# Head norms of the projection: one operand of every root step in PSUM

## The chip, the cores and the metric

The kernel runs on one core of a Trainium2 chip. That core has a matrix engine (TensorE, written PE; its weight loads PEld), three engines for element-wise work (VectorE = DVE, ScalarE = ACT, GpSimd = POOL), and an engine that mostly issues transfers (SyncE = SP). All work on SBUF, the core's large memory of 128 partitions; PE writes its results into PSUM, a small second memory of eight banks, which DVE and ACT can also read and write. The metric is the device time of one execution in microseconds; the kernel before takes 3017.64 us (median of 3 runs, 3017.33 to 3021.18).

## What is computed

One step of a two-layer network on 1024 latent tokens and 128 context tokens, with 1024 features each. Every layer has a normalisation with modulation, a projection `h @ w_in` into parts for a convolution branch and two attention branches, the three branches, an output projection and a two-step MLP. All of it is float32; the matrix products are made of three products of split operands, so that they keep about float32 precision.

The change touches one piece of that, the norm of each attention head. The projection's columns for queries and keys are cut into heads of 64, and each is divided by its root mean square:

```
def _rms(x, g):
    xf = x.astype(jnp.float32)
    y = xf * lax.rsqrt(jnp.mean(xf * xf, axis=-1, keepdims=True) + EPS)
    return (y * g.astype(jnp.float32)).astype(x.dtype)
...
    qa = _rms(qa.reshape(B, L, GQA_HEADS, HEAD_DIM), aqg)
    ka = _rms(ka.reshape(B, L, GQA_KV_HEADS, HEAD_DIM), akg)
    qn = _rms(qn.reshape(B, L, NA_HEADS, HEAD_DIM), nqg)
    kn = _rms(kn.reshape(B, L, NA_HEADS, HEAD_DIM), nkg)
```

## The kernel before

The program is written in one fixed order: each engine executes its instructions in the order in which the Python code emits them, and Python generators (`yield`, `next`) interleave the pieces by hand. A framework adds the semaphores between engines. Tiles come from pools: the pools S, T, U and V in SBUF, and eight PSUM buffers of one bank each (`P`), which are handed out again as they come free.

A layer begins with its norm (`norm1`), goes on to the projection (`project`), then the two attentions (`gqa`, `natten`), the output projection and the MLP. The projection works in column blocks of 256: V0 and V1 feed the convolution, A0 to A5 hold queries, keys and some values, VN values. Each of A0 to VN is walked in five token groups (`GROUPS`): four of two 128-token tiles (48 matmuls each) and one, the context tokens, of one tile (24 matmuls). For each group, in this order:

- PE multiplies (`tok_group`, L541 to L543) into a PSUM tile `pst`.
- In groups 1 and 3, the next weight half-block is split into a high and a low part (`wh` by ACT, `wl` by DVE), and another is fetched (`wr`).
- The first half of `post` calls `head_stats`: ACT squares (`sq`), DVE sums over each head (`ss`, L420), ACT takes Ln and Exp (`y`, by `rsq_start`). A tile of n = 2, 4 or 8 numbers per partition results.
- One step of the convolution follows (`conv_taps`): one or two taps on DVE (`cacc`, L102) for one half of the channels, and for the other half one tap by ACT (`cp`) and POOL (`cacc`, L570), from the end of block A1 on. POOL's part has 22 taps, DVE's the rest.
- The second half of `post` calls `head_norm`: three small DVE steps improve the root (`rsq_end`, through L102), one DVE multiplication applies it (`xn`, L99), and POOL multiplies by gains or rotates (`o`, L471 to L490).
- In every second group, one step of the modulation (`fill`) runs: PE multiplies a weight row block (`aw`) into `psmod`; when a modulation is complete, DVE copies `psmod` to `mt` (L229) and PE transposes it (`psmt`, L233).
- SP issues the transfers (all through L144): weights `wr`, modulation weights `aw`, and the stores of `o` to DRAM buffers (`ddA`, `dvA`), each three groups after it was noted.

The VN block has no head norm, so there are 30 norms in a layer and 60 in all. From block A5 on, the grouped attention's start is interleaved as well: it loads the keys back from DRAM (`kd`), and PE transposes them (`pstr`, L784).

The root is computed in two parts. `rsq_start` (ACT) makes y = exp(-0.5 ln(ss/64 + eps)), an approximate reciprocal root. `rsq_end` (DVE) makes one Newton step: t = y*y*(-0.5/64), t = (ss + 64 eps)*t, y = (t + 1.5)*y. All of y, t and ss are small tiles of pool V in SBUF. The same two helpers serve the other norms, which the change leaves alone.

Of the kernel before, what the change touches and what calls it, by code (L numbers as in the profile page):

```python
# [14 lines left out]
ACTF = mybir.ActivationFunctionType  # L15
ALU = mybir.AluOpType
# [9 lines left out]
DH = 64  # L26
EPS = 1e-6
# [18 lines left out]
def hybrid_step(ctx, tc, I, O, depth=DEPTH):  # L46
# [7 lines left out]
    def nm(p):  # L54
        count[0] += 1
        return f"{p}{count[0]}"
# [4 lines left out]
    def T(shape, dt=F32, n="t"):  # L61
        return pers.tile([128] + list(shape), dt, tag="T", bufs=N_T, name=nm(n))
# [4 lines left out]
    def V(shape, n="v"):  # L67
        return pers.tile([128] + list(shape), F32, tag="V", bufs=24, name=nm(n))
# [18 lines left out]
    def P(n="ps"):  # L87
        return psum.tile([128, 512], F32, tag="p", bufs=8, name=nm(n))
# [3 lines left out]
    def act(out, in_, func, scale=1.0, bias=0.0, **k):  # L92
        nc.scalar.activation(out=out, in_=in_, func=func, scale=scale, bias=bias, **k)  # L93
# [4 lines left out]
    def tt(out, a, b, op, eng=None):  # L98
        (eng or nc.vector).tensor_tensor(out=out, in0=a, in1=b, op=op)  # L99

    def stt(out, a, s, b, op0, op1):
        nc.vector.scalar_tensor_tensor(out=out, in0=a, scalar=s, in1=b, op0=op0, op1=op1)  # L102
# [7 lines left out]
    eps = pers.tile([128, 1], F32, name="eps")  # L110
# [51 lines left out]
    def rsq_start(q, y, m):  # L162

        act(y, q, ACTF.Ln, scale=1.0 / m, bias=eps)
        act(y, y, ACTF.Exp, scale=-0.5)

    def rsq_end(q, y, t, m):

        stt(t, y, -0.5 / m, y, ALU.mult, ALU.mult)
        stt(t, q, EPS * m, t, ALU.add, ALU.mult)  # L170
        stt(y, t, 1.5, y, ALU.add, ALU.mult)
# [239 lines left out]
    def heads4(a, nt):  # L411

        return a.rearrange("p t (h d) -> p t h d", d=64)

    def head_stats(x, nt):
        n = nt * (x.shape[2] // 64)
        sq = T([nt, x.shape[2]], n="sq")
        act(sq, x, ACTF.Square)
        ss = V([n], "ss")
        nc.vector.tensor_reduce(out=ss, in_=sq.rearrange("p t (h d) -> p (t h) d", d=64), op=ALU.add, axis=AX.X)  # L420
        y = V([n], "y")
        rsq_start(ss, y, DH)
        return x, nt, n, ss, y

    def head_norm(x, nt, n, ss, y):
        rsq_end(ss, y, V([n], "nt"), DH)
        w = x.shape[2]
        xn = T([nt, w], n="xn")
        tt(heads4(xn, nt), heads4(x, nt), y.rearrange("p (t h) -> p t h", t=nt).unsqueeze(3).to_broadcast([128, nt, w // 64, 64]), ALU.mult)
        return xn  # L430
# [61 lines left out]
    def post(L, c, t, nt, ps):  # L492
# [5 lines left out]
        if normed is not None:  # L498
            st = head_stats(x[:, :, normed], nt)
# [4 lines left out]
        if normed is not None:  # L504
            xn = head_norm(*st)
            if c in ("A0", "A1"):
                post_rope(L, c, t, nt, xn, o)
            else:
                gain(o[:, :, normed], xn, 2 if c in ("A2", "A3") else 3, nt, L)
# [1463 lines left out]
```

## Time and profile before

| what | value |
|---|---|
| median of 3 runs | 3017.64 us |
| the profiled execution's own time | 3022.51 us |
| its span, first to last instruction | 3020.7 us |
| mean granted TensorE clock | 0.972 |
| busy PE / DVE / ACT / POOL | 2857.6 / 2085.0 / 1403.4 / 650.5 us |
| projection of layer 0, about 109 to 345 us: busy PE / DVE / ACT / POOL | 221.3 / 176.5 / 80.4 / 148.4 us |
| projection of layer 1, about 1610 to 1845 us: busy PE / DVE / ACT / POOL | 221.3 / 180.4 / 81.2 / 143.0 us |

All durations and places come from the one profiled execution; its own time stands 4.87 us above the median of the others. A row of a timeline has the start, the duration, the engine, the line and the operation, the tile written and the tiles read, the shapes and, in brackets, the idle time before it with what ended that. L93, L96, L99, L102 and L106 are helpers (activation, ACT copy, two-operand step, scalar-and-two-tensor step, tensor-scalar step), so the tile's name tells which work it is. In lists of waits, the first name is who waited and the second what ended the wait.

### The profile page before, as it was taken

How to read it: one execution, taken by the hardware profiler on the slowest of the kernel's cores; microseconds unless marked ns; L12 is line 12 of the kernel's file. 1: busy time of each engine (PE TensorE's matmuls, PEld its weight loads, DVE VectorE, ACT ScalarE, POOL GpSimd, SP SyncE). 2: the span in 40 equal slices, each digit the busy share in tenths (PEclk: the TensorE clock that was granted, in tenths of full speed). 3: DMA queues.
4: the chain of work that ended last, by engine and by line, in shares of the span. 5: the costliest groups of instructions: out<-in, count | busy, mean ns of one | idle time of the engine just before them, and what ended most of it. 6: DMA issues, size and time to landing. Idle time of an engine off the chain costs nothing.

```text
span 3020.7 us, 52765 instructions
## 1 busy us (share of the span) xinstructions
PE 2857.6 (95%) x20328; PEld 2540.2 (84%) x20328; DVE 2085.0 (69%) x3985; ACT 1403.4 (46%) x2880; POOL 650.5 (22%) x607
## 2 busy tenths in 40 slices
PE   6998999999889999999889999999997999999999
PEld 3878745799789999999878886458997999999999
DVE  6587778864767556758665877778557775585676
ACT  4334356763644444433452343568435444434344
POOL 3576345410000000000225762463100000000000
PEclk7999999999999999999989999999998999999999
DMA  7276302423466658443433671024334654575334
GB/s 282 82 209 172 97 24 55 101 81 114 134 197 200 207 165 297 162 154 95 139 122 98 186 205 59 16 59 105 95 119 155 194 174 158 174 253 175 126 96 164
DMA packets 424124, 430.42 MB, mean 142 GB/s; under 512 B 120000, under 2 KB 299968, under 8 KB 423872
## 3 DMA queue, kind: packets, MB, share of 16 engines
q1 hardware_dynamic: 423872, 427.04, 45.4%
q8 instruction: 160, 2.62, 0.4%
q14 instruction: 92, 0.75, 0.1%
HBM read 298.50 MB, written 128.45 MB: 141 GB/s over the span
## 4 chain that ended last, share of the span: by engine, by line
PE 74%; DVE 14%; ACT 4%; DMA 2%; issue 2%; POOL 2%; SPq 1%; DVEq 0%; POOLq 0%; ACTq 0%
PE ps L1319 23%; PE psa L1319 8%; PE psc L1319 7%; PE pso L1319 5%; PE psb L1319 5%; PE psacc L1118 3%; PE pspv L985 2%; DVE cacc L102 2%; PE psd L1319 2%; PE pspt L969 2%; PE psst L1132 2%; PE psm L1044 2%; PE pst L541 1%; PE pst L542 1%; PE pst L543 1%
## 5 line engine op out<-in xcount | busy, mean ns | idle before, releaser
L1319 PE MATMUL ps<-ts,w2h 128*128 128x288 f32 x3072 | 534.4, 296 | 8.3 <-DVE ts L99 4.8
L1319 PEld LDWEIGHTS ps<-ts,w2h 128*128 128x128 f32 x3072 | 451.7, 189 | 9.2 <-DVE ts L99 5.3
L1319 PE MATMUL ps<-ts,w2l 128*128 128x288 f32 x1536 | 329.2, 295 | 0.1
L96 ACT CAST ts<-ti 128x576 fp32r<-128x576 f32 x256 | 172.1, 672 | 314.4 <-PE ps L1319 216.4
L541 PE MATMUL pst<-wh,HA 128*128 128x256 f32 x1040 | 298.8, 287 | 0.0
L542 PE MATMUL pst<-wl,HA 128*128 128x256 f32 x1040 | 295.8, 284 | 0.0
L543 PE MATMUL pst<-wh,HA 128*128 128x256 f32 x1040 | 294.7, 283 | 0.0
L93 ACT ACTIVATE ev<-ev 128x576 f32<-128x576 f32 x224 | 153.7, 686 | 275.0 <-DVE ev L99 271.4
L1319 PEld LDWEIGHTS ps<-ts,w2l 128*128 128x128 f32 x1536 | 247.4, 189 | 0.4 <-DVE w2l L99 0.3
L99 DVE TENSOR_TENSOR ts<-ti,ts 128x576 fp32r<-128x576 f32 x256 | 194.6, 760 | 48.4 <-ACT ts L96 47.6
L102 DVE SCALAR_TENSOR_TENSOR X<-ps,mod,X 128x288 f32<-128x288 f32 x336 | 112.1, 408 | 161.4 <-PE ps L1319 161.4
L541 PEld LDWEIGHTS pst<-wh,HA 128*128 128x128 f32 x1040 | 199.6, 192 | 19.8 <-issue 7.6
L542 PEld LDWEIGHTS pst<-wl,HA 128*128 128x128 f32 x1040 | 199.3, 192 | 0.1
L543 PEld LDWEIGHTS pst<-wh,HA 128*128 128x128 f32 x1040 | 199.3, 192 | 0.0
L99 POOL TENSOR_TENSOR nacc<-nacc,nsq 128x512 f32<-128x512 f32 (+1 forms) x12 | 15.9, 1322 | 836.4 <-PE ps L1319 810.4
L1762 POOL COPY yu<-X 128x128 f32<-128x128 f32 x8 | 3.9, 499 | 855.2 <-DVE X L102 843.2
L99 DVE TENSOR_TENSOR w1l<-w1r,w1h 128x512 fp32r<-128x512 f32 x128 | 87.7, 689 | 133.6 <-ACT w1h L96 130.2
L1319 PE MATMUL pso<-HA,woh 128*128 128x288 f32 x1024 | 177.6, 295 | 0.0
L1046 DVE TENSOR_REDUCE mx<-psm 128x1 f32<-128x384 f32 x288 | 142.2, 546 | 31.9 <-PE psm L1044 31.7
L93 ACT ACTIVATE pt<-psst 128x512 f32<-128x512 f32 x216 | 118.2, 597 | 90.9 <-PE psst L1133 89.9
L99 POOL TENSOR_TENSOR R<-R,pt 128x1024 f32<-128x1024 f32 x60 | 148.3, 2472 | 27.9 <-ACT pt L93 25.9
L1319 PEld LDWEIGHTS pso<-HA,woh 128*128 128x128 f32 x1024 | 149.6, 188 | 0.0
(279 smaller groups left out, 7290.2 us busy)
## 6 DMA issues: line engine op xcount, KB each, us to landing
ti<-hd SPq DMA_DIRECT2D x128, 576.0 KB, 4.0
hd<-ev SPq DMA_DIRECT2D x224, 288.0 KB, 3.8
aw<-in_ada_w SPq DMA_DIRECT2D x160, 256.0 KB, 3.8
w1r<-in_mlp_w SPq DMA_DIRECT2D x160, 256.0 KB, 4.4
HF<-in_mlp_w SPq DMA_DIRECT2D x128, 256.0 KB, 5.1
ddA<-o SPq DMA_DIRECT2D x144, 128.0 KB, 2.9
wr<-in_w_in SPq DMA_DIRECT2D x28, 512.0 KB, 4.0
qd<-ddA SPq DMA_DIRECT2D x48, 256.0 KB, 3.3
```

The lines of the kernel that those rows point to most:

```text
L93: nc.scalar.activation(out=out, in_=in_, func=func, scale=scale, bias=bias, **k)
L96: nc.scalar.copy(out, in_)
L99: (eng or nc.vector).tensor_tensor(out=out, in0=a, in1=b, op=op)
L102: nc.vector.scalar_tensor_tensor(out=out, in0=a, scalar=s, in1=b, op0=op0, op1=op1)
L541: mm(o, hi, wh, start=(k == 0), stop=False)
L542: mm(o, hi, wl, start=False, stop=False)
L543: mm(o, lo, wh, start=False, stop=(k == KT - 1))
L969: nc.tensor.transpose(ps[0:n, c], self.p[j][:, o:o + n], ident)
L985: mm(ps[64 * j:64 * j + 64, 0:128], v[j], self.at[j, i], start=(i == 0), stop=(i == nb - 1))
L1046: nc.vector.tensor_reduce(out=mx[j][:, qt, b:b + 1], in_=ps[:, 0:384], op=ALU.max, axis=AX.X)
L1118: mm(acc[64 * j:64 * j + 64, :], v, pt[:, j, :], start=(kt == 0), stop=(kt == 8))
L1319: mm(ps[h][:, 0:HH], x, y[:, h * HH:(h + 1) * HH], start=(start and z == 0), stop=(stop and z == 2), skip_group_check=True)
```

## The change

`head_stats` and `head_norm` no longer use the two helpers. `head_stats` takes one more PSUM buffer (`pss`) and cuts two small pieces from it, z and t. ACT computes the approximate root twice from the same logarithm: into z in PSUM and into y in SBUF. The three DVE steps are the same arithmetic with other operands: t (PSUM) from y (SBUF) and z (PSUM); z (PSUM) from ss (SBUF) and t (PSUM); y (SBUF) from z (PSUM) and y (SBUF). The V tile `nt` goes away.

```
         y = V([n], "y")
-        rsq_start(ss, y, DH)
-        return x, nt, n, ss, y
-
-    def head_norm(x, nt, n, ss, y):
-        rsq_end(ss, y, V([n], "nt"), DH)
+        small = P("pss")
+        z, t = small[:, 0:n], small[:, 64:64 + n]
+        act(y, ss, ACTF.Ln, scale=1.0 / DH, bias=eps)
+        act(z, y, ACTF.Exp, scale=-0.5)
+        act(y, y, ACTF.Exp, scale=-0.5)
+        return x, nt, n, ss, y, z, t
+
+    def head_norm(x, nt, n, ss, y, z, t):
+
+        stt(t, y, -0.5 / DH, z, ALU.mult, ALU.mult)
+        stt(z, ss, EPS * DH, t, ALU.add, ALU.mult)
+        stt(y, z, 1.5, y, ALU.add, ALU.mult)
         w = x.shape[2]
```

## The prediction

> **What bounds the kernel now.** I first read the busy time of each engine over the two projection stages, where all 60 head norms run, 30 in each layer.
>
> ```profile
> 109.00:345.00 236.00, 221.34 (x1741) 198.55 (x1739) 176.45 (x238) 80.41 (x164) 148.42 (x118) 0.97 0.62 169
> 1610.00:1845.00 235.00, 221.28 (x1711) 195.01 (x1710) 180.37 (x243) 81.21 (x163) 143.04 (x113) 0.97 0.61 166
> ```
>
> After the stretch and its length stand the busy times of PE, PEld, DVE, ACT and POOL, then the granted clock. PE is busy for 221 of 235 us: TensorE is the bound, and DVE time counts only where it makes PE wait. So I asked next what PE waited for in these stretches (total, times, longest), layer 0 and then layer 1.
>
> ```profile
> PE psmod L224 <- DMA aw<-in_ada_w: 5.8, 5, 1.9
> PE psmt L233 <- DVE mt L229: 5.7, 1, 5.7
> PE pstr L784 <- DMA kd<-ddA: 3.1, 1, 3.1
> ```
>
> ```profile
> PE psmt L233 <- DVE mt L229: 5.5, 1, 5.5
> PE psmod L224 <- DMA aw<-in_ada_w: 3.3, 4, 1.6
> PE pstr L784 <- DMA kd<-ddA: 2.6, 1, 2.6
> ```
>
> That is 14.6 us and 11.4 us: in each layer one long wait for a DVE copy (mt, the modulation result), one for the first keys read back (kd), and short ones for modulation weights (aw). Behind the two long ones PE runs slowly for a while:
>
> ```profile
> 245.20:249.30 4.10, 4.10 (x20) 4.10 (x21) 3.95 (x6) 1.84 (x4) 0.61 (x2) 0.50 0.60 128
> 249.40:253.50 4.10, 4.10 (x37) 4.10 (x36) 4.07 (x4) 1.78 (x5) 4.10 (x2) 1.00 0.02 6
> 291.20:297.10 5.90, 5.90 (x28) 5.90 (x29) 2.48 (x6) 4.18 (x7) 3.98 (x3) 0.50 1.04 297
> 1739.40:1744.30 4.90, 4.90 (x24) 4.90 (x25) 4.74 (x8) 1.94 (x4) 1.35 (x2) 0.50 0.50 107
> 1785.40:1788.70 3.30, 3.30 (x16) 3.30 (x17) 2.46 (x6) 1.69 (x4) 1.81 (x2) 0.50 1.00 290
> ```
>
> At clock 0.50, 20 matmuls fit into the 4.1 us that hold 37 at clock 1.00 (0.111 us each). The four slow stretches therefore lose 4.1-20x0.111 = 1.9, 5.9-28x0.111 = 2.8, 4.9-24x0.111 = 2.2 and 3.3-16x0.111 = 1.5 us. They follow the mt, kd, mt and kd waits.
>
> **The change, part by part.** The three steps of the root now take all tensor inputs from SBUF. The listings by tile show what such steps cost (minimum/median/maximum in ns):
>
> ```profile
> L93 ACT ACTIVATE y<-y x60: 203/208/211, 119.7 to 1804.7; 128x8 f32<-128x8 f32 x32, 128x4 f32<-128x4 f32 x24, 128x2 f32<-128x2 f32 x4
> L102 DVE SCALAR_TENSOR_TENSOR nt<-y x60: 146/168/2690, 122.7 to 1804.9; 128x8 f32<-128x8 f32 x32, 128x4 f32<-128x4 f32 x24, 128x2 f32<-128x2 f32 x4
> L99 DVE TENSOR_TENSOR xn<-pst,y x60: 290/690/693, 123.2 to 1809.6; 128x512 f32<-128x512 f32 x32, 128x256 f32<-128x256 f32 x24, 128x128 f32<-128x128 f32 x4
> L99 DVE TENSOR_TENSOR mod<-psmt,vecs x12: 156/164/174, 46.1 to 1854.9; 128x16 f32<-128x16 f32 x12
> L102 DVE SCALAR_TENSOR_TENSOR A<-mod,vecs x8: 151/166/2116, 46.3 to 1857.1; 128x8 f32<-128x8 f32 x8
> L102 DVE SCALAR_TENSOR_TENSOR rt<-rr,pssum x12: 670/676/687, 398.4 to 2067.0; 128x512 f32<-128x512 f32 x12
> L102 DVE SCALAR_TENSOR_TENSOR cacc<-cin,vecs,cacc x78: 1417/1450/3710, 135.7 to 1853.5; 128x1167 f32<-128x1167 f32 x78
> ```
>
> A norm step of 0.165 us sometimes takes 2.7. So do other steps with two SBUF inputs: A, and the convolution taps cacc. Steps with one PSUM input never do: xn runs right behind the norm and never passes 0.693, mod keeps to 0.156-0.174, and rt is the changed steps' own instruction with SBUF first and PSUM second. The cause stands in the timeline, DVE and then POOL:
>
> ```profile
> 280.23 1.54 DVE L102 SCALAR_TENSOR_TENSOR nt<-y 128x4 f32<-128x4 f32 x1 [0.60 <-ACT y L93]
> 281.80 1.21 DVE L102 SCALAR_TENSOR_TENSOR nt<-ss,nt 128x4 f32<-128x4 f32 x1
> 283.05 2.63 DVE L102 SCALAR_TENSOR_TENSOR y<-nt,y 128x4 f32<-128x4 f32 x1
> 285.81 0.42 DVE L99 TENSOR_TENSOR xn<-pst,y 128x256 f32<-128x256 f32 x1
> ```
>
> ```profile
> 279.05 2.70 POOL L570 TENSOR_TENSOR cacc<-cacc,cp 128x1167 f32<-128x1167 f32 x1 [1.33 <-DMA aw<-in_ada_w]
> 281.71 1.28 POOL L471 TENSOR_TENSOR o<-xn,gains 128x512 f32<-128x512 f32 x1
> 282.95 2.71 POOL L570 TENSOR_TENSOR cacc<-cacc,cp 128x1167 f32<-128x1167 f32 x1
> ```
>
> Each step ends just as a POOL instruction ends: three POOL instructions, three steps. How much that is, by the busy time of the norm steps alone, in layer 0's projection and in the stretch before its mt wait:
>
> ```profile
> 109.00:345.00 236.00, 47.44 (x90) 0.97 0.62 169
> 209.00:239.40 30.40, 11.93 (x12) 1.00 0.55 154
> ```
>
> Unstalled, 90 steps take 90x0.165 = 14.9 us; the other 32.5 us are stall, in layer 0 alone. The change takes this off DVE; from PE it takes nothing by itself.
>
> *Added.* One Exp into PSUM per norm. Into SBUF it takes 0.21 us; an Exp written to PSUM is not in the trace. In order behind the other Exp it lengthens the chain by 0 to 0.21 us; I take 0.15, nearest to the SBUF row. ACT is busy for 80 of 236 us, so this hides in its waiting time; were ACT full, it would cost 60x0.21 = 12.6 us. The DVE steps' price in PSUM: the nearest rows are mod (0.164, one PSUM input) and A (0.166, none), so 0 +- 0.02 us each, at most 180x0.02 = 4 us of DVE, on no path of PE.
>
> The Trainium skill's Perfetto Trace Analysis (Optimizing Scalar/DVE Operations) puts DVE's fixed access cost at about 60 ns in SBUF and 125 ns in PSUM, which speaks against the change: as an estimate, 180x65 ns would put 11.7 us more on DVE. The rows mod and A show no such difference in the length of an instruction.
>
> *The mt wait.* The work of DVE just before it, and the taps' busy time by themselves up to there (DVE's is 15.48 us for 8 taps, POOL's 14.99 for 5):
>
> ```profile
> 237.28 5.84 DVE L102 SCALAR_TENSOR_TENSOR cacc<-cin,vecs,cacc 128x1167 f32<-128x1167 f32 x2
> 244.29 0.68 DVE L229 COPY mt<-psmod 128x512 f32<-128x512 f32 x1
> ```
>
> ```profile
> 209.00:244.40 35.40, 0.00 (x0) 0.00 (x0) 15.48 (x8) 0.00 (x0) 14.99 (x5) 0.97 0.54 145
> ```
>
> An unhindered tap takes 1.43 us, so 8 need 11.5 and wait 4.0. The 12 norm steps wait 11.93-12x0.165 = 9.9. Without that, DVE reaches the next tap, or the next weight split wl, earlier; these keep two SBUF inputs and will meet POOL in its place. Following the order by hand, with POOL's tap at 2.7 us, its gain at 1.3 and the waiting engine next in turn, taps and splits wait about 6 us in place of 4. DVE is then 9.9-2 = 8 us earlier at mt, and 5.7 are enough. So I take the whole wait off, 5.7 and 5.5, and the slow clock behind it, 1.9 and 2.2: **15.3 us**. Bounds: 0 if the taps take back all of it, 15.3 if they take back under 4.
>
> *The kd wait.* The norm quoted at 280.23 takes 5.4 instead of 0.55 us, so its xn comes 4.9 earlier. SP issues in order, and its loads and stores wait for such an xn and for POOL's outputs behind it:
>
> ```profile
> 277.74 2.15 SPq L144 DMA_DIRECT2D ddA<-o  x4
> 279.99 3.36 SPq L144 DMA_DIRECT2D aw<-in_ada_w  x4
> 283.40 2.80 SPq L144 DMA_DIRECT2D ddA<-o  x4
> 286.30 0.62 SPq L144 DMA_DIRECT2D kd<-ddA  x1
> ```
>
> ```profile
> 1777.21 2.20 SPq L144 DMA_DIRECT2D ddA<-o  x4
> ```
>
> In layer 0 the 3.36 and 2.80 can shrink to 2.15, what four issues took just before. Then kd leaves 1.9 us earlier, and the slow clock (2.8) goes with most of the wait. In layer 1 the issues ahead of kd are hardly hindered (2.20 for four); I take 1.0 of the 2.6 and keep the slow clock. **5.7 us**; bounds 0 and 3.1+2.8+2.6+1.5 = 10.0.
>
> *The aw waits* (9.1 us) lie mostly where the stalls are still short. I take **1 us**; bounds 0 and 9.1.
>
> Sum: 15.3+5.7+1 = 22 us off the profiled execution's own 3022.51, 3000.5. That execution stood 4.87 above the median of the runs, 3017.64; against the median the forecast is **2996**.
>
> *PSUM.* One more of 8 buffers per norm, held until its third step; psmod holds one throughout. Seven buffers at two per group still let PE be three groups ahead of the norms. I cost it at nothing; its price if that is wrong is rival (d).
>
> **Rivals.**
>
> (a) *The stall moves to the taps.* DVE leaves the norm early and stands as long in the next tap or split. For it: the pair at 237.28 already loses 5.84-2.86 = 3.0 us. Against: a norm meets POOL up to three times, a pair of taps twice. With half of the mt wait kept and all its slow clock, 11.2/2+1 = 7 us are gained: 3011. The Trainium skill's SBUF — State Buffer (Who interferes with whom) has the shared port locked for a whole instruction, this rival's mechanism; the timeline above agrees.
>
> (b) *All three waits go*, because SP and POOL come as early as DVE: 15.3+10.0+6 = 31 us, 2986. Against: SP issues back to back in layer 1.
>
> (c) *No effect*: PE's waits follow POOL's taps and SP's issues and only DVE's idle time grows, or a PSUM input does not free the steps: 3018. For it: POOL is busy for 148 of 236 us, and the stores wait for it. Against: mt waits for DVE alone.
>
> (d) *Slower: PE waits for a PSUM buffer.* If only two groups' worth turn over, PE may start a group only when the norm of the last but one is done. A group of two tiles is 48 matmuls, 5.3 us. The norm would run some 7 us behind it (an estimate: Square, sums, Ln and Exp 2, taps 2.9, their wait 1, steps and xn 1.2), so 1.7 us for each of the 32 such groups in blocks A1 to A4 of both layers: 54 us, less the 22, 3050. It decides once a norm runs further behind than one group. Against: the lists of PE's waits hold no wait for a buffer.
>
> **How the numbers follow.** Forecast 0.54, (a) 0.16, (b) 0.12, (c) 0.10, (d) 0.08. A measurement of this kernel tells about 0.2%, 6 us, from no change. Faster: the forecast, (b) and most of (a), 0.79. Within 0.2%: (c) and the rest of (a), 0.13. Slower: 0.08. The range runs from (b) with a little more of the aw waits to just past (a), 2982 to 3014; (c) and (d) lie outside.
>
> **What would show it.** Norm steps never over 0.25 us and their 47 us in layer 0 near 15; longer means on cacc and wl; the psmt waits gone and clock 1.00 where they were; layer 0's kd wait below 1.5 us. If norm steps still reach 2.6 us, a PSUM input does not free DVE and the forecast falls. If they are short and psmt still waits over 3 us, it is (a) or (c). If the weight loads of pst wait for DVE and the projection grows, it is (d).

## The result, and the profile after

The changed kernel takes **2996.61 us** (median of 4 runs, 2994.11 to 3002.31); the kernel before, timed beside it, 3019.41 us (4 runs, 3017.33 to 3024.02). The ratio is 0.9925, with a 95% interval of 0.9906 to 0.9944: a gain of 22.8 us. The forecast was 22 us off the 3017.64 us of the three earlier runs of before, that is 2996. The time is right; the experiments show that one of the steps to it was not.

The profiled execution of the changed kernel has a time of its own of 2996.72 us and a span of 2994.9; that of before, 3022.51 and 3020.7. Compare first the two projections, from the first to the last matrix product of the blocks. Before, by stretches: length, then busy PE, PEld, DVE, ACT and POOL, then the granted clock.

```profile
109.30:343.90 234.60, 219.94 (x1731) 198.13 (x1730) 175.57 (x238) 80.04 (x163) 148.42 (x118) 0.97 0.62 170
1603.80:1837.20 233.40, 221.96 (x1731) 198.31 (x1729) 176.95 (x239) 81.29 (x164) 148.14 (x118) 0.97 0.61 166
```

After:

```profile
107.20:328.20 221.00, 215.87 (x1730) 193.51 (x1729) 147.69 (x238) 86.18 (x193) 150.46 (x118) 1.00 0.66 180
1588.00:1808.10 220.10, 215.00 (x1731) 194.21 (x1729) 148.15 (x239) 87.17 (x194) 152.79 (x118) 1.00 0.65 176
```

Layer 0's projection is 13.6 us shorter and layer 1's 13.3, together 26.9. The same number of matmuls keeps PE busy for 4.1 us less in layer 0 and for 7.0 less in layer 1. Most of that is the slow clock, which is gone (0.97 to 1.00). By the working of the prediction its four stretches cost 1.9+2.8 = 4.7 us in layer 0 and 2.2+1.5 = 3.7 in layer 1. Layer 1 had a third stretch, behind short waits for aw:

```profile
1645.40:1648.80 3.40, 3.35 (x6) 0.17 (x4) 3.18 (x5) 1.44 (x3) 3.32 (x4) 0.51 0.92 226
```

At half the clock it loses 1.7 of its 3.4 us. Another 1.6 of the 7.0 us are not placed. The rest of the gain, 9.5 and 6.3 us, is PE idle before (234.60-219.94 = 14.7 and 11.4) that is not idle any more (5.1 and 5.1). The prologue, which the change does not touch, was 2.1 us shorter in this execution: from 88 to 93 us the granted clock was 0.66 in the profile of before and is 1.00 here. The kernel before without POOL's taps (one of the experiments below), whose prologue is the same as before, also has 1.00 there, so this is not the change's doing. 26.9+2.1 less the 25.8 between the spans leaves 3.2 us given back after layer 1's projection. Of the 25.8, 3.1 come from the profiled execution of before standing above its median here (3022.51 against 3019.41).

One profiled execution against one other is therefore rough by a few us. The closest neighbour of the changed kernel is the first experiment below, the same instructions with z and t in SBUF. Its projections take 231.8 and 231.6 us (107.5 to 339.3 and 1602.5 to 1834.1), and the changed kernel's are 22.3 us shorter than these: 8.8 us of busy PE and 13.5 us of idle PE.

The waits of PE in the projections after (total, times, longest), layer 0, then layer 1:

```profile
PE psmod L224 <- DMA aw<-in_ada_w: 4.5, 6, 1.5
PE psnm L1042 <- DVE nmx L1036: 2.3, 1, 2.3
PE pstr L791 <- DMA kd<-ddA: 0.7, 1, 0.7
```

```profile
PE psmod L224 <- DMA aw<-in_ada_w: 4.5, 4, 1.5
PE psmu L736 <- DVE cacc L102: 3.2, 1, 3.2
PE psnm L1042 <- DVE nmx L1036: 2.3, 1, 2.3
PE pstr L791 <- DMA kd<-ddA: 0.6, 1, 0.6
```

The wait at mt (psmt, 5.7 and 5.5) has left both lists, kd is down from 3.1 and 2.6 to 0.7 and 0.6, and aw stands at 9.0 in all (9.1 before). The waits named psnm and psmu belong to the start of attention.

The norm steps by themselves, in the two projections (DVE, then ACT's new Exp), and by tile (minimum/median/maximum in ns):

```profile
107.00:340.00 233.00, 14.81 (x90) 5.37 (x30) 0.99 0.63 174
1590.00:1825.00 235.00, 14.83 (x90) 5.36 (x30) 0.99 0.62 169
```

```profile
L93 ACT ACTIVATE pss<-y x60: 175/180/181, 117.6 to 1775.8; 128x8 f32<-128x8 f32 x32, 128x4 f32<-128x4 f32 x24, 128x2 f32<-128x2 f32 x4
L102 DVE SCALAR_TENSOR_TENSOR pss<-y,pss x60: 151/162/172, 120.5 to 1776.2; 128x8 f32<-128x8 f32 x32, 128x4 f32<-128x4 f32 x24, 128x2 f32<-128x2 f32 x4
L102 DVE SCALAR_TENSOR_TENSOR pss<-ss,pss x60: 165/170/173, 120.7 to 1776.4; 128x8 f32<-128x8 f32 x32, 128x4 f32<-128x4 f32 x24, 128x2 f32<-128x2 f32 x4
L102 DVE SCALAR_TENSOR_TENSOR y<-pss,y x60: 159/166/166, 120.9 to 1776.6; 128x8 f32<-128x8 f32 x32, 128x4 f32<-128x4 f32 x24, 128x2 f32<-128x2 f32 x4
```

None of 180 steps passes 0.173 us, where some took 2.7; layer 0's 47.4 us became 14.8. DVE is now idle, by the first table, for 73 of 221 us in layer 0. Around mt the timeline of DVE reads:

```profile
229.46 3.41 DVE L102 SCALAR_TENSOR_TENSOR cacc<-cin,vecs,cacc 128x1167 f32<-128x1167 f32 x2
232.79 0.16 DVE L102 SCALAR_TENSOR_TENSOR pss<-y,pss 128x8 f32<-128x8 f32 x1
...
234.05 0.68 DVE L229 COPY mt<-psmod 128x512 f32<-128x512 f32 x1
```

mt is copied at 234.05 in place of 244.29, and the pair of taps ahead of it takes 3.41 us in place of 5.84.

### The profile page after: what moved, and what is told of

It is laid out like the page before. It is cut to its first block, busy times and chain, and to the rows that moved or that the text cites. A ratio compares the mean times of both kernels' runs of the same rounds, so it can differ in the third digit from the quotient of the medians.

```text
span 2994.9 us, 52825 instructions
## 1 busy us (share of the span) xinstructions
PE 2843.5 (95%) x20328; PEld 2529.8 (84%) x20328; DVE 2030.1 (68%) x3985; ACT 1416.0 (47%) x2940; POOL 656.1 (22%) x607
## 4 chain that ended last, share of the span: by engine, by line
PE 77%; DVE 10%; ACT 4%; POOL 3%; DMA 2%; issue 2%; SPq 1%; DVEq 0%; POOLq 0%; ACTq 0%
PE ps L1326 23%; PE psa L1326 8%; PE psc L1326 7%; PE pso L1326 5%; PE psb L1326 5%; PE psacc L1125 3%; PE pst L548 3%; PE pst L549 3%; PE pst L550 3%; PE pspv L992 2%; PE psd L1326 2%; PE pspt L976 2%; PE psst L1139 2%; PE psm L1051 1%; PE pstr L791 1%
## 5 line engine op out<-in xcount | busy, mean ns | idle before, releaser
L548 PE MATMUL pst<-wh,HA 128*128 128x256 f32 x1040 | 295.3, 284 | 0.0
L550 PE MATMUL pst<-wh,HA 128*128 128x256 f32 x1040 | 291.7, 280 | 0.0
L548 PEld LDWEIGHTS pst<-wh,HA 128*128 128x128 f32 x1040 | 195.8, 188 | 19.2 <-PE pst L550 5.2
L550 PEld LDWEIGHTS pst<-wh,HA 128*128 128x128 f32 x1040 | 196.0, 188 | 0.0
L102 DVE SCALAR_TENSOR_TENSOR cacc<-cin,vecs,cacc 128x1167 f32<-128x1167 f32 x78 | 138.5, 1775 | 18.6 <-POOL cacc L577 17.4
```

What stands on the lines that cost most here:

```text
L548: mm(o, hi, wh, start=(k == 0), stop=False)
L550: mm(o, lo, wh, start=False, stop=(k == KT - 1))
```

## The experiments

Each kernel was timed beside the kernel before; the ratio is to that. They undo one part of the change, do one part alone, or price one wait. The short diffs are against the changed kernel, except where the text says that a kernel is made from the one before.

### The change with z and t in SBUF

```
-        small = P("pss")
-        z, t = small[:, 0:n], small[:, 64:64 + n]
+        z, t = V([n], "z"), V([n], "tn")
```

> The change as it is, but z and t are two small SBUF tiles instead of pieces of a PSUM buffer; the second Exp and the order of the steps stay. Theory (a step with two SBUF inputs waits for POOL, one with a PSUM input does not): the stall is back, norm steps again reach 2.6 to 2.7 us and sum to about 47 us in a projection, PE waits 5 to 6 us for mt in each layer, and the time is that of the kernel before, 3014 to 3022 us. Rival (the gain comes from the new form of the chain, a separate z and t instead of steps in place): norm steps stay near 0.17 us and the time near 2997 us.

Measured: 3020.85 against 3020.31, ratio 1.0004 (0.9994 to 1.0013). The same instructions in the same order, but for the place of two small tiles, gain nothing. The stall is back, a little smaller than expected: the norm steps take 42.9 us in layer 0 and 43.9 in layer 1, PE waits 4.0 and 3.8 us at mt and 4.0 and 2.5 at kd, and the longest step is again 2675 ns:

```profile
L102 DVE SCALAR_TENSOR_TENSOR tn<-y,z x60: 148/278/2675, 120.8 to 1802.4; 128x8 f32<-128x8 f32 x32, 128x4 f32<-128x4 f32 x24, 128x2 f32<-128x2 f32 x4
```

The place in PSUM is the whole gain.

### The new Exp alone

```
-        stt(t, y, -0.5 / DH, z, ALU.mult, ALU.mult)
-        stt(z, ss, EPS * DH, t, ALU.add, ALU.mult)
-        stt(y, z, 1.5, y, ALU.add, ALU.mult)
+        rsq_end(ss, y, V([n], "nt"), DH)
```

> Only what the change adds: the second Exp into a PSUM buffer is made and read by nobody, and the three steps are those of the kernel before, in SBUF. Theory: ACT has room, so 60 more instructions of about 0.18 us (11 us of ACT) cost nothing on PE's path: 3015 to 3023 us, with the mt and kd waits as before. Rival (the longer chain delays every norm, and the change gained more than was seen): 3 to 10 us slower than before, up to 3029 us.

Measured: 3020.93, ratio 0.9999 (0.9990 to 1.0008). The Exp into PSUM, 0.18 us each, costs nothing that can be measured.

### Blocks A0 to A3 alone, and A4 and A5 alone

Two kernels; in the second the list is `("A4", "A5")`. The other blocks keep the old steps.

```
+        if not new:
+            rsq_start(ss, y, DH)
+            return x, nt, n, ss, y, None, None
...
+        if z is None:
+            rsq_end(ss, y, V([n], "nt"), DH)
+        else:
...
-            st = head_stats(x[:, :, normed], nt)
+            st = head_stats(x[:, :, normed], nt, c in ("A0", "A1", "A2", "A3"))
```

> The change in blocks A0 to A3 alone, the old steps in A4 and A5. Theory (time is gained only at the waits of PE behind which the stall stands): the mt waits (5.7 and 5.5 us) and the slow clock behind them (1.9 and 2.2 us) go, the kd waits stay at 2 to 3 us: 15 us gained, 3000 to 3007 us. Rival (kd waits for the whole backlog of DVE and SP, not for block A4's norms): the kd waits go as well, below 1 us, and the time is near 2997 us.

> The change in blocks A4 and A5 alone, the old steps in A0 to A3. Theory: the mt waits stay at 5 to 6 us in each layer with clock 0.50 behind them, the kd waits fall below 1 us and the clock behind them is 1.00: about 2.4+2.0+2.8+1.5 = 9 us gained, 3008 to 3013 us; with the run on A0 to A3 it adds up to the change's 23 us. Rival (kd follows the backlog from the earlier blocks): the kd waits stay above 2 us and the time within 3 us of the kernel before.

Measured: A0 to A3 give **2998.62**, ratio 0.9924 (0.9912 to 0.9935), the whole gain and more than the theory allowed; A4 and A5 give 3021.30, ratio 1.0004 (0.9995 to 1.0013), nothing, though their norm steps do not stall any more (0.172 us at most). With A4 and A5 alone kd is issued at 283.66, 2.6 us earlier than before, and yet PE stands 2.9 us in front of the same transposes (put down there to the norm's xn) and then 3.1 us for the last taps (psmu), a wait that the profile of before does not have in layer 0. The step of the prediction that took 5.7 us at kd from the stall of one norm of A4 (quoted at 280.23) falls. DVE, then POOL and SP, in layer 0 with only A0 to A3 changed:

```profile
269.81 1.54 DVE L102 SCALAR_TENSOR_TENSOR nt<-y 128x4 f32<-128x4 f32 x1 [0.60 <-ACT y L93]
271.38 1.21 DVE L102 SCALAR_TENSOR_TENSOR nt<-ss,nt 128x4 f32<-128x4 f32 x1
272.63 2.62 DVE L102 SCALAR_TENSOR_TENSOR y<-nt,y 128x4 f32<-128x4 f32 x1
275.37 0.42 DVE L99 TENSOR_TENSOR xn<-pst,y 128x256 f32<-128x256 f32 x1
```

```profile
271.29 1.28 POOL L484 TENSOR_TENSOR o<-xn,gains 128x512 f32<-128x512 f32 x1
...
272.98 2.36 SPq L144 DMA_DIRECT2D ddA<-o  x4
275.43 1.70 SPq L144 DMA_DIRECT2D kd<-ddA  x1
```

The norm stalls exactly as before, 5.4 us, but the stores ahead of kd leave at 272.98, before the norm's xn at 275.37: they do not wait for this norm. What they follow is POOL's gain for an earlier group, which ends at 272.57, 10.4 us earlier than before (281.71+1.28 = 282.99); kd is issued 10.9 us earlier (275.43 against 286.30) and PE waits for it 1.8 us in place of 3.1, and not at all in layer 1. The rows of the prediction could have said so: there, too, the stores at 283.40 begin before that norm's xn at 285.81. kd is set by how late the earlier blocks left DVE and POOL.

### Blocks A2 and A3 alone, and A3 alone

The same edit with `c in ("A2", "A3")`, and with `c == "A3"`.

> The change made in blocks A2 and A3 alone (10 of the 30 norms of a layer); A0, A1, A4 and A5 keep the old steps. In layer 0 before, DVE is busy for only 3.6 of the 10 us from 190 to 200 us, which is in A2's first two groups, and over 95% from there to the wait at mt. Theory: a stall counts only if DVE has no idle time between it and the place where PE waits, so A0's and A1's stalls (4.4 us over 10 norms) are made good anyway and A2 and A3 (16.3 us) bring all of the gain: 2996 to 3001, no wait at mt. Rival: every stall ahead of the wait counts alike, 16.3 of 20.7 us: a gain of 17 of 21.7 us, 3002 to 3006, with some wait left at mt or kd.

> The change made in block A3 alone: 5 norms of a layer, of which three lie ahead of the wait at mt in layer 0 and stall 5.1 us there; A2's five norms with 7.8 us of stall keep the old steps. Theory: stalls count in proportion once DVE has no idle time: 5.1 us removed, one or two taken back by taps and wl, leave 1.5 to 3 us of wait at mt and some of the wait at kd: 3004 to 3012. Rival: a few us are all it takes, and A3 brings the whole gain: 2995 to 3001.

Measured: A2 and A3 **2995.67** against 3019.80, ratio 0.9912 (0.9897 to 0.9928); A3 alone **3003.21** against 3020.44, ratio 0.9947 (0.9934 to 0.9959); each lies just below the lower end of its theory. So 10 of the 30 norms of a layer bring all of the gain; A0 and A1, ahead of a stretch in which DVE is busy for 3.6 of 10 us, need no change. Five norms bring 17 us. Their waits in layer 0's projection (then the start of attention), A2 and A3 first, A3 alone second:

```profile
PE psmod L224 <- DMA aw<-in_ada_w: 3.3, 3, 1.7
PE psnm L1048 <- DVE nmx L1042: 2.3, 1, 2.3
PE pstr L797 <- DMA kd<-ddA: 1.7, 1, 1.7
```

```profile
PE psmod L224 <- DMA aw<-in_ada_w: 5.3, 6, 1.7
PE pstr L797 <- DMA kd<-ddA: 2.7, 1, 2.7
...
PE psmt L233 <- DVE mt L229: 0.9, 1, 0.9
```

With A3 alone the wait at mt of 5.7 us shrinks to 0.9 and kd stays at 2.7; with A2 as well, mt goes and kd falls to 1.7. The first microseconds taken off DVE's delay serve mt, the next ones kd. The slow clock behind kd shrinks already with A3 alone: about 3.4 us at 0.50 in layer 0, none in layer 1. In medians that is 17.2 us with A3 alone (12 to 20 by its interval), and 5 to 7 more with A2 or with the whole change.

### The wait at mt taken away by itself

The kernel before, with the transposes of mt issued one step of the modulation later; what follows them in the modulation, the clearing of the next psmod first of all, moves a step later with them:

```
             nc.vector.tensor_copy(mt, ps)
             yield
+            if not first:
+                yield
             pt = P("psmt")
```

> The kernel before, norm steps untouched (they stall as before); only the transposes of mt on PE are issued one step of the modulation later (some 10 us), so PE does not stand at mt. Theory: the wait at mt is where DVE's delay first reaches PE; DVE, ACT and POOL stay as late as they were, so without that stop PE arrives about 5.6 us earlier at the keys (kd) and waits there for most of what it saved: kd waits 3.1 -> 6 to 9 us and 2.6 -> 5 to 8 us, time 3013 to 3019. Rival (the sum of my prediction, which priced each wait by itself): the mt wait and its slow clock go, kd stays near 3, time 3003 to 3008.

Measured: 3024.26 against 3019.80, ratio 1.0009 (0.9998 to 1.0019). No gain, against a sum that prices each wait by itself (3003 to 3008). The time lies above the theory's range too, and PE did not stop where the theory put it. Layer 0's projection:

```profile
PE psmod L224 <- DVE psmod L219: 10.1, 1, 10.1
PE psmod L224 <- DMA aw<-in_ada_w: 4.7, 5, 1.8
```

DVE around the place:

```profile
268.57 0.90 DVE L102 SCALAR_TENSOR_TENSOR nt<-y 128x8 f32<-128x8 f32 x1 [0.61 <-ACT y L93]
269.51 1.20 DVE L102 SCALAR_TENSOR_TENSOR nt<-ss,nt 128x8 f32<-128x8 f32 x1
270.74 2.57 DVE L102 SCALAR_TENSOR_TENSOR y<-nt,y 128x8 f32<-128x8 f32 x1
273.41 0.69 DVE L99 TENSOR_TENSOR xn<-pst,y 128x512 f32<-128x512 f32 x1
274.21 0.48 DVE L219 MEMSET psmod<- 128x512 f32 x1
```

PE runs past mt and stops at the next thing it needs from DVE, the clearing of the next psmod, for 10.1 us in place of 5.7; in layer 1 it stops at a weight split (wl, 5.7) and at psmod (2.7). kd does not grow (no wait in layer 0, 2.0 us in layer 1), since DVE's delay is met ahead of it. The wait at mt is a symptom: the delay on DVE is what costs, and it is paid at the next handover.

### Only the first step with an operand in PSUM

```
-        stt(t, y, -0.5 / DH, z, ALU.mult, ALU.mult)
-        stt(z, ss, EPS * DH, t, ALU.add, ALU.mult)
-        stt(y, z, 1.5, y, ALU.add, ALU.mult)
+        v = V([n], "nt")
+        stt(v, y, -0.5 / DH, z, ALU.mult, ALU.mult)
+        stt(v, ss, EPS * DH, v, ALU.add, ALU.mult)
+        stt(y, v, 1.5, y, ALU.add, ALU.mult)
```

> Only the first of the three norm steps keeps an operand in PSUM (it reads z there); the second and third read and write SBUF again. In the kernel before, the three steps of layer 0's projection took 19.8, 11.2 and 16.4 us, unhindered 5 us each. Theory: a step waits for the POOL instruction that runs beside it, so what step 1 no longer waits for, step 2 meets instead; only the POOL instruction that would have been met first is sometimes over by then. Norm steps 36 to 46 us in layer 0 (before 47.4, after 14.8), the wait at mt stays between 2 and 5 us, time 3008 to 3018. Rival: the steps wait independently of each other, so the first one's 14.9 us of stall just go: norm steps 32 to 34 us, the wait at mt under 1.5 us, time 3000 to 3007. Full gain (2996) would say that one PSUM operand is enough.

Measured: 3016.03 against 3019.80, ratio 0.9985 (0.9975 to 0.9996). The time and the wait at mt (3.2 and 2.9 us) are the theory's, the length of the steps (33.0 us in layer 0) is the rival's. DVE's groups in layer 0 (busy, mean ns):

```profile
L99 DVE TENSOR_TENSOR wl<-wr,wh 128x1024 fp32r<-128x1024 f32 x12 | 23.0, 1917 | 4.1 <-ACT wh L96 3.9
L102 DVE SCALAR_TENSOR_TENSOR nt<-ss,nt 128x8 f32<-128x8 f32 (+2 forms) x30 | 19.5, 651 | 1.0
L102 DVE SCALAR_TENSOR_TENSOR y<-nt,y 128x8 f32<-128x8 f32 (+2 forms) x30 | 8.9, 298 | 1.0
L102 DVE SCALAR_TENSOR_TENSOR nt<-y,pss 128x8 f32<-128x8 f32 (+2 forms) x30 | 4.6, 153 | 9.0 <-ACT y L93 9.0
```

The second step now stalls as the first one did (19.5 us; the first took 19.8 before, and the second 11.2): the stall is displaced by one step. The third step fell from 16.4 to 8.9 us. The three steps lose only 14.4 us together, and little of that reaches PE. An operand in PSUM for the first step alone is not enough; whether two of the three would do was not run.

### POOL's taps left out

The kernel before without POOL's additions, so that the output lacks those taps. They are 21 in a layer (the first of POOL's 22 taps is made by ACT alone):

```
                 act(p, cin[:, k:k + CW], ACTF.Copy, scale=dww(L.l, j, k))
-                nc.gpsimd.tensor_tensor(out=acc[:, 0:CW], in0=acc[:, 0:CW], in1=p, op=ALU.add)
```

> The kernel before with the old norm steps, but without the additions of the convolution's taps on POOL (22 per layer; ACT still forms the products, which nobody reads; the output lacks these taps). POOL's gains and rotary products stay. It tests the cause of the stalls. In layer 0 before, the stalled steps that end with a POOL tap lose 25.7 us, those that end with a gain or a table product 5.9 us. Theory: POOL's instructions are the cause, so norm steps fall from 47.4 to 18 to 24 us, the DVE taps from 65.7 to 55 to 60 us, and the wait at mt goes: 2985 to 2998. Rival: the stalls come from elsewhere (ACT's writes, the transfers) and only happen to end with POOL's instructions: norm steps above 40 us, 3012 to 3020.

Measured: 2992.10 against 3020.44, ratio 0.9903 (0.9888 to 0.9917). The three old steps, all in SBUF, in layer 0:

```profile
L102 DVE SCALAR_TENSOR_TENSOR y<-nt,y 128x8 f32<-128x8 f32 (+2 forms) x30 | 7.1, 236 | 1.0
L102 DVE SCALAR_TENSOR_TENSOR nt<-y 128x8 f32<-128x8 f32 (+2 forms) x30 | 7.0, 235 | 6.6 <-ACT y L93 6.6
L102 DVE SCALAR_TENSOR_TENSOR nt<-ss,nt 128x8 f32<-128x8 f32 (+2 forms) x30 | 5.7, 190 | 1.0
```

Together 19.8 us in place of 47.4, with DVE's own code unchanged: POOL's instructions are what the steps wait for. The DVE taps fell from 65.7 to 59.9 us, and of the wait at mt 0.3 us is left in layer 0 and nothing in layer 1, both as the theory had it. The Trainium skill's SBUF — State Buffer (Who interferes with whom) says that a DVE instruction with two SBUF inputs contends with a GpSimd instruction that reads SBUF, and that one with at most one SBUF input, outside the 2-port perf modes, does not contend with GpSimd. These runs agree with both: a norm step took up to 2.7 us with two SBUF inputs and at most 0.173 with one.

### Two PSUM buffers per norm

```
-        small = P("pss")
-        z, t = small[:, 0:n], small[:, 64:64 + n]
+        z, t = P("pss")[:, 0:n], P("pst2")[:, 0:n]
```

> The changed kernel, with z and t in two PSUM buffers per norm instead of one, so that a group takes three of the 8 buffers (psmod holds one throughout). It prices rival (d), the turnover of buffers. Theory: a norm runs 8 to 13 us behind its group and a group of PE takes 5.9, so with three buffers to a group PE is held now and then, by a few us per layer (the changed kernel shows 2.6 us in all): 2997 to 3006. Rival (d): PE may start a group only when the norm of the last but one is done: a microsecond or more in most of the 40 groups of blocks A1 to A4, 3010 to 3050.

Measured: 3011.69 against 3020.44, ratio 0.9974 (0.9963 to 0.9984), 15 us above the changed kernel's median: above the theory, and at the low end of rival (d), but not by its mechanism. PE waits once in each layer for the buffer of a late norm, 3.1 us; in layer 0:

```profile
PE psmod L224 <- DMA aw<-in_ada_w: 7.7, 6, 2.6
PE pst L547 <- DVE pss L102: 3.1, 1, 3.1
...
PE pstr L790 <- DVE pst L102: 1.9, 1, 1.9
```

The stops at pss and in front of the keys (pstr, put down here to a norm step and not to kd) add 4.3 us to the changed kernel's waits in layer 0, aw another 3.2, and the clock dips again (0.99 over each projection). Not each group is held, only one in each layer; but one buffer more per norm gives back over half of the gain.

### DVE's spare time spent: the last taps a step earlier

Once POOL's taps are all issued, two DVE taps per step and not two and one in turn, on the changed kernel and on the kernel before:

```
-            for _ in range(2 if n <= 6 else 1 + n % 2):
+            for _ in range(2 if n <= 6 or not p else 1 + n % 2):
```

> The changed kernel, with two DVE taps in every step once POOL's taps are all issued (before: two and one in turn), so that the last tap is issued one step earlier. The changed kernel waits 3.2 us for the last pair of taps at the start of attention in layer 1, and in layer 0 PE stands 3.2 us at the same place. Theory: DVE now has time to spare in the last projection blocks (about 28 us per layer), so the taps fit there without delaying a norm, both waits go: 6.4 us less, 2989 to 2993. Rival: the taps meet POOL one step earlier and push the norms or wl by as much, or another wait (nmx, kd) follows: 2994 to 3000.

> The kernel before, with the same earlier taps that brought the changed kernel from 2996.6 to 2979.3 us (two DVE taps in every step once POOL's are all issued). It tells whether that gain needs the DVE time that the change sets free. Theory: it does not; the taps lie behind the waits for mt and kd, and the waits for psmu, psst and psnm at the start of attention go all the same: a gain of 8 to 17 us, 3003 to 3012. Rival: with norm steps that stall for up to 2.7 us, one more tap per step delays the norms of A5 and the keys, and the gain is eaten: 3015 to 3022.

Measured: on the changed kernel **2979.34** against 3019.80, ratio 0.9857 (0.9839 to 0.9875); on the kernel before **2999.81** against 3020.44, ratio 0.9928 (0.9915 to 0.9941). The first lies below both of its ranges by some 10 us, the second just below its theory's. Neither needs the other: 0.9925 x 0.9928 = 0.9854. The changed kernel waited at the start of both attentions for the last taps and for work queued behind them on DVE, over the whole execution:

```profile
PE psnm L1042 <- DVE nmx L1036: 10.2, 6, 2.5
...
PE psmu L736 <- DVE cacc L102: 6.4, 2, 3.2
PE psst L1139 <- DVE mx L1053: 5.7, 2, 2.9
```

With the earlier taps, the psmu and the psst wait are gone; this stands in their place:

```profile
PE psnm L1042 <- DVE nmx L1036: 8.8, 4, 2.3
...
PE pssum L1091 <- DVE R L99: 1.8, 2, 0.9
PE psvr L749 <- DVE lsq L99: 1.7, 2, 0.9
```

That is 6.4+5.7+1.4-1.8-1.7 = 10.0 us of the 12.4 between the two profiled spans (2994.9 and 2982.5). I had counted the psmu wait alone; the maximum (mx) that PE waited for behind it was late for the same taps. This list of waits is not the whole account: in the same pair the projections grew by 5.5 us, and the stretches behind them shrank by 18.0. The median fell by 5 us more than the span; this profiled execution stood at 2984.25, above its median. On the kernel before, the waits at mt (5.7 and 5.9) and kd (3.5 and 2.5) stay as they were, which is why the two gains add. This version beats both kernels.

## Why the prediction was right, and where it was not

**The norm steps: right.** 47.4 to 14.8 us, never over 0.25; the length of a step with an operand in PSUM lay within the 0.02 us given. **The Exp: nearly.** It takes 0.18 us and lengthens the chain by about 0.21, the whole of my upper bound, where I took 0.15: a first step that waited 0.60 for ACT (the row at 280.23) now waits 0.82.

```profile
264.95 0.17 DVE L102 SCALAR_TENSOR_TENSOR pss<-y,pss 128x8 f32<-128x8 f32 x1 [0.82 <-ACT y L93]
```

The cover held, since the Exp alone lost nothing.

**The mt wait: right, and the largest term.** Forecast 15.3 us; A3's norms alone, which take the wait down to 0.9 and leave PE's wait at kd at 2.7, are worth 17.2, part of that through the slow clock behind kd. But I priced the wait as if taking it away were enough. It is not: moved out of the way, PE stood 10.1 us at the next psmod. The term held because the change removes what makes DVE late. What taps and splits take back before mt was put at 2 us, and that was wrong: the eight taps took 13.6 us there in place of 15.5, and one split (wl) 2.45 in place of 1.22, so that nothing was taken back on balance. Over the whole stage the mean of the taps stayed at 1.72 us in layer 0 (1.72 before), and it is the weight splits that grew, from 19.4 to 23.6 us (11 each). Rival (a) had half of the mt wait left; none is.

**The kd wait: the step is wrong, the size too small.** "The norm quoted at 280.23 takes 5.4 instead of 0.55 us, so its xn comes 4.9 earlier" is true of the norm and not what sets kd: A4 and A5 alone gain nothing, and with A0 to A3 alone that norm stalls as before while kd leaves 10.9 us earlier. Most of the cause is the delay that DVE and POOL carry from A2 and A3: with these alone the kd waits fall from 3.1 and 2.6 to 1.7 and 1.6 us. In layer 1, where I took 1.0 us and kept the slow clock, the wait fell by 2.0 and the slow clock went.

**The slow clock: undersized.** Of my four stretches I took three, 1.9+2.8+2.2 = 6.9 us, as won; PE's busy time fell by 4.1+7.0 = 11.1 us. In layer 0 it was a little less than forecast, 4.1 against 4.7. Layer 1 had more than the two stretches I quoted: the one behind kd, which I kept, and a third behind a wait for aw. These make 5.4 of the 7.0 us there; the rest is open.

**The aw waits: nothing**, 9.1 to 9.0, where I took 1 us.

**PSUM: right as built, with little to spare.** At one buffer per norm PE shows no wait that matters; at two, 15 us come back. Rival (d) misjudged how: one group of each layer is held, not all 16.

**The sum.** In the profiled pair the projections gained 26.9 us for a forecast of 22: 15.8 us of idle PE, where 11.2+2.9+1 = 15.1 were forecast, and 11.1 us of busy PE, where 6.9 were. Against the same instructions with z and t in SBUF they gained 22.3, as 13.5 and 8.8; there the waits at mt were 7.8 us and not 11.2, and those at kd 6.5 and not 5.7. So the sum stands better than its split, which differs by a few us from one profile to the next. The medians differ by 22.8, since the profiled execution of before was a long one and 3.2 us were given back later; so the exact time owes something to errors that cancel. Rival (b) was right that kd goes almost entirely, and wrong on aw; (a) and (c) were not seen. What stays open: why the aw waits did not move, and 1.6 us of PE's busy time in layer 1.

## What to carry to other kernels

Price the delay, not the wait: find the engine that is late, go back from the wait to where that engine was last idle, and count only the stalls between; here 10 of 30 norms carried the whole gain, and A0, A1, A4 and A5 carried none. Before blaming a norm for a late transfer, compare start times: a store that is issued before the norm's output exists does not wait for it. Where short DVE steps stall beside POOL, give every one of them in the row an operand in PSUM, since one on the first step alone displaced the stall here, and count the PSUM buffers first.

## What the runs showed of the hardware that was not expected

An Exp of the same shape is shorter into PSUM than into SBUF: 0.180 us (pss<-y) against 0.208, both for y<-y and for the same instruction with z in SBUF (z<-y in the first experiment). The Trainium skill's Perfetto Trace Analysis (Optimizing Scalar/DVE Operations) has the same sign for the scalar engine, about 93 ns against 51; the difference here is 28 ns. For DVE it says 60 against 125 ns; the three steps differ by 0.008 us at most between themselves and from the 0.165 of an unstalled step in SBUF, so nothing of that shows in their length.
